# Adding four of the five feed-forward down chunks onto x inside PSUM, with ScalarE carrying x in and out

## The chip, the cores and the metric

One core of a Trainium2 chip. TensorE (PE) multiplies matrices into PSUM banks, VectorE (DVE) and ScalarE (ACT) work on tiles of 128 partitions in SBUF and PSUM, GpSimd (POOL) and SyncE (SP) mainly issue transfers. The metric is the time of one execution on the device in microseconds (us).

## The reference

A trunk of two layers over 512 tokens of width 1024. Each layer adds three things to `x`: a mixer, a memory cross-attention and a convolutional feed-forward part.

```
def conv_ffn(xn, w_up, conv_w, conv_b, w_down):
    h = causal_depthwise_conv(xn @ w_up, conv_w) + conv_b
    g, u = jnp.split(h, 2, axis=-1)
    return (jax.nn.gelu(g) * u) @ w_down

x = x + conv_ffn(rms_norm(x, ffn_norm[layer]), ...)
```

`w_up` is 1024 x 5632, `w_down` is 2816 x 1024. All is float32.

## The kernel before

`x` is kept transposed in SBUF as eight tiles `self.x[m]`, 128 features by 512 tokens each. A product of float32 precision is made of three matmuls on operands that are split into a high and a low part (`mm3`, lines 291 to 293). The split of a weight tile costs a ScalarE cast (the high part `wh`) and a VectorE subtraction (the low part `wl`).

The feed-forward part (`ffn_steps`) makes the 2816 inner features as 22 pairs of 128 gate and 128 up features. Most pairs go through `seven`: seven half products with 256 columns instead of eight (a Strassen-like scheme), whose intermediate sums sit in the PSUM banks `acc`, `y` and `s`. Between these products ScalarE carries sums from bank to bank or to SBUF: `seed` (line 1774) opens bank Y with the negative of X, `kept` (line 1778) saves two sums, lines 1791 and 1798 copy two quarters of the result out; VectorE makes the other two by a subtraction (line 1781). `tail` then applies the convolution (ScalarE line 1657, VectorE line 1664), the gelu (line 1672), the product of gate and up (line 1674) and the split of the result into `ah` (line 1678, ScalarE) and `al`. These activations stay in SBUF.

The down projection takes them in five chunks of pairs, `CHUNKS = [(0, 4), (4, 4), (8, 4), (12, 4), (16, 6)]`. As soon as a chunk of pairs is there, eight blocks `down(c, m)`, one for each output tile `m`, are put in a queue, and `fill()` takes one from it at two places of each later pair. A block loads its weights (`dr`, 256 KB), splits them (line 1554), runs 4 x 3 matmuls of 512 columns into one of the two banks `w`, and VectorE adds the bank onto `self.x[m]` (`xadd`, line 619). Pairs 0 to 4 have no down blocks in between, nor have pairs 17, 20 and 21: the last five blocks of chunk 3 are kept back and run one after the other behind the last pair. In layer 0 the eight blocks of chunk 4 follow in the same manner, with six pairs each. In layer 1 chunk 4 is left to `finish`, which adds in its own way (line 2105), loads the table for a square root (line 2133), and norms and writes the output.

The order on every engine is planned in Python. `Sched.add` takes a task's engine, estimated time, dependencies, due time and the buffers that it takes and frees. `Sched.run` gives each engine in turn the task that can start first, and among those that can start at the same time the one with the lowest due time. `clock[0]` is the running sum of TensorE's estimated time, and due times are written relative to it. Estimated times are `act = lambda n: 0.1 + 0.83e-3 * n` on ScalarE and `tt = lambda n: 0.055 + 1.06e-3 * n` on VectorE. Buffers are taken in the order of the program; the resource `w` has two slots. A framework turns the resulting program into semaphore waits and may move instructions that are ready ahead of others that are not. Each engine executes its own queue in order.

Due times that matter here: a block's weight cast at `at - 3.0`, where `at` is the clock at the block's start; the addition at the clock after the block plus 3.0; the seed of bank Y at the clock at a pair's start plus 1.5; the convolution at the clock after the pair plus 5.0 (3.0 handed to `tail`, which adds 2.0).

Of the kernel before, what the change touches and what calls it, by code (L numbers as in the profile page):

```python
# [40 lines left out]
OFF = 16  # L41
# [24 lines left out]
class Plan:  # L66
# [11 lines left out]
    def add(self, fn, dur=0.0, deps=(), prio=None, take=(), free=(), chain=(), pre=(), after=0.0, order=(), load=(), st=None):  # L78
        it = Item(fn, dur, [d for d in deps if d is not None], len(self.items) if prio is None else prio, take, free, chain, pre, after, order, load, st)
        it.n = len(self.items)  # L80
        self.items.append(it)
        return it
# [154 lines left out]
class Builder:  # L237
# [185 lines left out]
    def xs(self):  # L423
        return self.xh, self.xl
# [1082 lines left out]
    def ffn_steps(self, layer, mp):  # L1507
# [3 lines left out]
        nc, t = self.nc, self.t  # L1511
        sc = Sched(raw=3, h=3, s2=1, s4=1, a22=1, sa=3, sb=2, ra=2, hs=2, c=1, dr=2, u2=1, u5=1, act=10, acc=2, y=2, s=2, w=2)
        add = sc.add
        tt = lambda n: 0.055 + 1.06e-3 * n
        act = lambda n: 0.1 + 0.83e-3 * n
        ACV, STT = 0.71, 0.66
        clock = [0.0]
# [5 lines left out]
        def pe(dur, fn, deps, take=(), free=()):  # L1523
            clock[0] += dur
            return add("PE", dur, fn, deps, clock[0] - dur, take, free, 0.2)

        def joined(deps, prio, free):
            return add("-", 0.0, None, deps, prio, (), free, 0.0)
# [18 lines left out]
        def weight(src, cols, at, tag="raw", off=0):  # L1547

            st = {"apart": 0}
            l = load(st, tag, src, cols, at - 9.0)  # L1550

            def hi():
                st["wh"], st["wl"] = (self.til(self.wp, i, (P, 1088), F32R, bufs=3)[:, off:] for i in ("wh", "wl"))
                nc.scalar.copy(st["wh"][:, :cols], st[tag][:, :cols])  # L1554

            def low():
                n, end = st["apart"], cols - P
                for a, b, c in ((0, end, 0), (end, cols, n)) if n else ((0, cols, 0),):
                    self.sub(st["wl"][:, a + c : b + c], st[tag][:, a:b], st["wh"][:, a:b])

            def rows(k):
                s, n = slice(k * P, (k + 1) * P), k * P + (st["apart"] if (k + 1) * P == cols else 0)
                return st["wh"][:, s], st["wl"][:, n : n + P]

            st["rows"] = rows
            h = add("ACT", act(cols), hi, [l], at - 3.0, [("h", st)])
            lo = add("DVE", tt(cols), low, [h], at - 2.0, (), [(tag, st)])
            return st, lo

        def block(src, nk, xs, at, bank, deps, steps, tag="raw", off=0):  # L1570

            st, lo = weight(src, nk * P, at, tag, off)
            last = None
            per = nk // steps
            for c in range(steps):

                def fn(c=c):
                    if c == 0:
                        st["ps"] = self.bank(bank) if bank == "w" else self.acc_bank(st["_acc"] if bank == "acc" else 2 + st["_y"])
                    for k in range(c * per, (c + 1) * per):  # L1580
                        self.mm3(st["ps"][:], *st["rows"](k), *xs(k), k == 0, k == nk - 1)

                last = pe(0.7 * per, fn, [lo, last, *deps], [(bank, st)] if c == 0 else (), [("h", st)] if c == steps - 1 else ())
            return st, last

        blk = lambda k: 2 * (k % 4) + k // 4
# [33 lines left out]
        formed = []  # L1620
# [70 lines left out]
        def plain(p, fill):  # L1691
            st = {}
            at = clock[0]
            get = rows(st, at + 5.0)
            ready = []
            for j in range(2):
                b, last = block(t["up"][layer, 22 * j + p], KB8, own, clock[0], ("acc", "y")[j], (), 2)
                last.block, b["step"] = b, (16, 32)[layer]

                def evac(j=j, b=b):  # L1700
                    nc.vector.tensor_tensor(out=st["hs_"][:, j, 2:514], in0=b["ps"][:], in1=self.rb, op=ALU.mult)

                if p == 0 and j == 0:
                    nonlocal normed
                    normed = norm()
                ready.append([add("DVE", 0.6, evac, [last, get, normed], clock[0] + 2.0, (), [(("acc", "y")[j], b)])])
                fill()
            tail(p, st, ready, clock[0] + 3.0)
# [102 lines left out]
        xadded = [None] * 8  # L1811
        queue, late = [], []

        def down(c, m, steps=1):
            first, nk = CHUNKS[c]
            d, last = block(
                t[f"down{c}"][layer, m], nk, lambda k: tuple(a[:] for a in acts[first + k]), clock[0], "w", [acted[first + k] for k in range(nk)], steps,
                "dr" if nk == 4 else "raw", OFF,
            )
            last.block, d["step"] = d, 16  # L1820
            if m == 7:
                for k in range(nk):
                    joined([last], last.prio, [("act", acted[first + k].st)])
            e = add("DVE", 0.6, lambda: self.xadd(m, d["ps"]), [last, xadded[m], *formed], clock[0] + 3.0, (), [("w", d)])
            xadded[m] = e
            return e

        def fill():
            nonlocal queue
            if queue:  # L1830
                down(*queue.pop(0))
# [15 lines left out]
        if layer == 0:  # L1847
            for m in range(8):
                e = down(4, m, 2)
                a = add("ACT", 1.2, lambda m=m: self.xprep(m, "mix", 1, state), [e], clock[0] + 3.0)  # L1850
                add("DVE", 1.3, None, [a], clock[0] + 3.0)
# [428 lines left out]
```

## Time and profile before

| | |
|---|---|
| median of 3 runs | 1461.26 us (1460.26 to 1461.54) |
| profiled execution, its own time | 1460.51 us |
| its span, first to last instruction | 1458.2 us |
| mean granted TensorE clock | 0.999 |
| TensorE busy, weight loads busy | 1441.9 us, 1279.6 us |
| VectorE, ScalarE, GpSimd busy | 1258.1 us, 930.4 us, 74.8 us |
| additions onto x from a `w` bank (line 619) | 72, of 0.69 us |

The profile is one execution. Busy time is the time in which an engine had at least one instruction in work; matmuls overlap, so that TensorE can be busy throughout and still lose a little between two of them. PEld is the weight load of TensorE, which runs beside the matmuls. In rows of groups stand line, engine, operation, output and input tile, count, then busy us and mean ns, then the idle time of the engine before them and what ended it. In rows of the timeline stand start, duration, engine, line, operation, tiles and count.

### The profile page before, as it was taken

What the parts mean: (1) busy time and instruction counts of PE and PEld (TensorE: products, weight loads), DVE (VectorE), ACT (ScalarE), POOL (GpSimd) and SP (SyncE); (2) the same over time, 40 slices, a digit from 0 to 9 for tenths busy, and PEclk for the clock granted to TensorE, in tenths of its full rate; (3) what the DMA queues carried; (4) which work ended last, traced back from release to release, by engine and by line L of the source; (5) the groups of instructions that cost most, each with busy time, mean ns of one, the idle gap of its engine ahead of it and who ended that gap; (6) DMA issues with size and microseconds to landing.
All of it is one profiled execution on the core that took longest, in us unless ns stands there. A gap on an engine that the chain in (4) does not pass through costs nothing.

```text
span 1458.2 us, 24038 instructions
## 1 busy us (share of the span) xinstructions
PE 1441.9 (99%) x9019; PEld 1279.6 (88%) x9019; DVE 1258.1 (86%) x2284; ACT 930.4 (64%) x1655; POOL 74.8 (5%) x116
## 2 busy tenths in 40 slices
PE   9999999999999999999999999999999999999998
PEld 7888787998899999999888888889988999999987
DVE  7789987867899999999769988887779999999974
ACT  7689665655676656666447565566566766656654
POOL 0001120000000000000000100000000000000000
PEclk9999999999999999999999999999999999999999
DMA  5222336752245666562233331656314666565322
GB/s 200 87 74 73 121 119 206 168 171 85 95 137 153 172 172 159 154 159 71 84 101 109 116 102 65 212 136 187 131 51 121 163 172 175 152 167 152 102 68 77
DMA packets 70627, 190.23 MB, mean 130 GB/s; under 512 B 7520, under 2 KB 7520, under 8 KB 70512
## 3 DMA queue, kind: packets, MB, share of 16 engines
q1 hardware_dynamic: 62304, 161.38, 34.1%
q0 software_dynamic: 7200, 26.22, 10.8%
q8 instruction: 70, 1.15, 0.3%
q10 hardware_dynamic: 1008, 1.12, 0.2%
q14 instruction: 45, 0.37, 0.1%
HBM read 186.56 MB, written 2.13 MB: 129 GB/s over the span
## 4 chain that ended last, share of the span: by engine, by line
PE 74%; DVE 17%; ACT 4%; issue 3%; DMA 1%; POOL 0%; SPq 0%; DVEq 0%; ACTq 0%; POOLq 0%
PE acc L291 14%; PE acc L292 14%; PE acc L293 14%; PE w L291 5%; PE w L293 5%; PE w L292 5%; DVE wl L282 3%; DVE c L1664 3%; PE s L291 3%; PE s L293 3%; PE s L292 3%; PE acc L352 2%; PE acc L354 2%; PE acc L353 2%; DVE hs L1804 1%
## 5 line engine op out<-in xcount | busy, mean ns | idle before, releaser
L282 DVE TENSOR_TENSOR wl<-raw,wh 128x1024 fp32r<-128x1024 f32 (+3 forms) x181 | 214.4, 1185 | 31.2 <-ACT wh L285 28.1
L291 PE MATMUL acc<-xh,wh 128*128 128x256 f32 (+1 forms) x624 | 207.1, 332 | 0.1
L293 PE MATMUL acc<-xh,wl 128*128 128x256 f32 (+1 forms) x624 | 206.0, 330 | 0.1
L292 PE MATMUL acc<-xl,wh 128*128 128x256 f32 (+1 forms) x624 | 205.8, 330 | 0.0
L285 ACT CAST wh<-raw 128x1024 fp32r<-128x1024 f32 (+1 forms) x123 | 126.5, 1033 | 89.3 <-PE acc L292 46.8
L1664 DVE SCALAR_TENSOR_TENSOR c<-hs,vec,c 128x512 f32<-128x512 f32 x176 | 129.7, 755 | 7.2 <-ACT c L1657 5.9
L291 PEld LDWEIGHTS acc<-xh,wh 128*128 128x128 f32 x624 | 117.3, 188 | 12.0 <-ACT v L1901 0.6
L293 PEld LDWEIGHTS acc<-xh,wl 128*128 128x128 f32 x624 | 117.3, 188 | 11.9 <-DVE wl L282 0.5
L292 PEld LDWEIGHTS acc<-xl,wh 128*128 128x128 f32 x624 | 117.3, 188 | 11.6
L293 PE MATMUL w<-ah,wl 128*128 128x512 f32 x304 | 119.3, 392 | 0.0
L292 PE MATMUL w<-al,wh 128*128 128x512 f32 x304 | 118.7, 390 | 0.0
L291 PE MATMUL w<-ah,wh 128*128 128x512 f32 x304 | 118.6, 390 | 0.0
L1657 ACT ACTIVATE c<-hs,vec 128x512 f32<-128x512 f32 x88 | 69.3, 813 | 13.4 <-DVE hs L1804 11.8
L282 DVE TENSOR_TENSOR wl<-sa,wh 128x1024 fp32r<-128x1024 f32 x52 | 63.8, 1227 | 5.2 <-ACT wh L1735 3.2
L293 PEld LDWEIGHTS w<-ah,wl 128*128 128x128 f32 x304 | 57.1, 188 | 11.9
L292 PEld LDWEIGHTS w<-al,wh 128*128 128x128 f32 x304 | 57.1, 188 | 9.9
L291 PEld LDWEIGHTS w<-ah,wh 128*128 128x128 f32 x304 | 57.1, 188 | 9.8
L1735 ACT CAST wh<-sa 128x1024 fp32r<-128x1024 f32 x42 | 44.1, 1049 | 34.0 <-PE w L292 24.4
L619 DVE TENSOR_TENSOR x<-w,x 128x512 f32<-128x512 f32 x72 | 50.1, 696 | 18.0 <-PE w L293 17.8
L1554 ACT CAST wh<-dr 128x512 fp32r<-128x512 f32 x64 | 39.6, 618 | 39.0 <-issue 35.5
L1735 ACT CAST s<-sb 128x512 fp32r<-128x512 f32 x84 | 52.1, 620 | 18.7 <-PE s L293 14.7
L282 DVE TENSOR_TENSOR s<-sb,s 128x512 fp32r<-128x512 f32 x92 | 63.7, 692 | 0.3 <-ACT s L285 0.3
(533 smaller groups left out, 4643.8 us busy)
## 6 DMA issues: line engine op xcount, KB each, us to landing
raw<-in_up_dram SPq DMA_DIRECT2D x46, 512.0 KB, 3.4
sa<-in_up_dram SPq DMA_DIRECT2D x42, 512.0 KB, 3.8
sa<-in_up_dram POOLq DMA_DIRECT2D x42, 512.0 KB, 5.4
dr<-in_down_dram SPq DMA_DIRECT2D x64, 256.0 KB, 3.2
ra<-in_up_dram SPq DMA_DIRECT2D x42, 256.0 KB, 3.0
raw<-in_xk_dram SPq DMA_DIRECT2D x16, 512.0 KB, 3.4
raw<-in_wo_dram SPq DMA_DIRECT2D x16, 512.0 KB, 3.4
raw<-in_xv_dram SPq DMA_DIRECT2D x16, 512.0 KB, 3.4
```

The costliest lines, as they stand in the source:

```text
L282: self.nc.vector.tensor_tensor(out=lo, in0=v, in1=hi.bitcast(F32), op=ALU.subtract)
L285: self.nc.scalar.copy(hi, v)
L291: mm(out, wh, xh, start=first, stop=False, skip_group_check=parts)
L292: mm(out, wh, xl, start=False, stop=False, skip_group_check=parts)
L293: mm(out, wl, xh, start=False, stop=last, skip_group_check=parts)
L352: mm(ps, xh[k][:, ts], wh[:, ws], start=(k == 0), stop=False)
L353: mm(ps, xh[k][:, ts], wl[:, ws], start=False, stop=False)
L619: self.nc.vector.tensor_tensor(out=self.x[m][:], in0=ps[:], in1=self.x[m][:], op=ALU.add)
L1554: nc.scalar.copy(st["wh"][:, :cols], st[tag][:, :cols])
L1657: nc.scalar.activation(st["c_"][:, j, :], hs()[:, j, 2:514], AF.Identity, scale=self.col("cw", (layer * 3 + 2) * 44 + blk), bias=self.col( ...
L1664: nc.vector.scalar_tensor_tensor(out=c, in0=hs()[:, j, n : n + 512], scalar=w, in1=c, op0=ALU.mult, op1=ALU.add)
L1735: nc.scalar.copy(s["wh"][:, :cols], raw())
```

## The change

`block` gets an argument `onto`. With it, a ScalarE task opens the PSUM bank and copies `x[m]` into it before the block, all matmuls of the block accumulate (none has the start flag), and `down` ends with a ScalarE copy of the bank back into `x[m]` in place of VectorE's addition. This holds for chunks 0 to 3 except the first two blocks of each layer, `(0, 0)` and `(0, 1)`: 30 blocks in each layer. The bank is taken by the seed, earlier than by the first matmul. Chunk 4 keeps the addition on VectorE.

```diff
-        def block(src, nk, xs, at, bank, deps, steps, tag="raw", off=0):
+        def block(src, nk, xs, at, bank, deps, steps, tag="raw", off=0, onto=None):
 
             st, lo = weight(src, nk * P, at, tag, off)
             last = None
             per = nk // steps
+
+            def opened():
+                st["ps"] = self.bank(bank) if bank == "w" else self.acc_bank(st["_acc"] if bank == "acc" else 2 + st["_y"])
+
+            if onto is not None:
+                x, x_deps = onto
+
+                def seed():
+                    opened()
+                    nc.scalar.copy(st["ps"][:], x[:])
+
+                last = add("ACT", act(512), seed, x_deps, at - 1.5, [(bank, st)])
             for c in range(steps):
 
                 def fn(c=c):
-                    if c == 0:
-                        st["ps"] = self.bank(bank) if bank == "w" else self.acc_bank(st["_acc"] if bank == "acc" else 2 + st["_y"])
+                    if c == 0 and onto is None:
+                        opened()
                     for k in range(c * per, (c + 1) * per):
-                        self.mm3(st["ps"][:], *st["rows"](k), *xs(k), k == 0, k == nk - 1)
-
-                last = pe(0.7 * per, fn, [lo, last, *deps], [(bank, st)] if c == 0 else (), [("h", st)] if c == steps - 1 else ())
+                        self.mm3(st["ps"][:], *st["rows"](k), *xs(k), k == 0 and onto is None, k == nk - 1, onto is not None)
+
+                last = pe(0.7 * per, fn, [lo, last, *deps], [(bank, st)] if c == 0 and onto is None else (), [("h", st)] if c == steps - 1 else ())
             return st, last
...
         def down(c, m, steps=1):
             first, nk = CHUNKS[c]
+            onto = (self.x[m], [xadded[m]]) if c < 4 and (c, m) not in ((0, 0), (0, 1)) else None
             d, last = block(
                 t[f"down{c}"][layer, m], nk, lambda k: tuple(a[:] for a in acts[first + k]), clock[0], "w", [acted[first + k] for k in range(nk)], steps,
-                "dr" if nk == 4 else "raw", OFF,
+                "dr" if nk == 4 else "raw", OFF, onto,
             )
...
-            e = add("DVE", 0.6, lambda: self.xadd(m, d["ps"]), [last, xadded[m], *formed], clock[0] + 3.0, (), [("w", d)])
+            if onto is None:
+                e = add("DVE", 0.6, lambda: self.xadd(m, d["ps"]), [last, xadded[m], *formed], clock[0] + 3.0, (), [("w", d)])
+            else:
+                e = add("ACT", act(512), lambda: nc.scalar.copy(self.x[m][:], d["ps"][:]), [last, *formed], clock[0] + 1.0, (), [("w", d)])
             xadded[m] = e
             return e
```

## The prediction

> **What bounds the kernel now.** I read the page first, then the busy times by stage, then what TensorE waited for in the stage that the change touches, then the order of instructions in one of its periods and at its end.
>
> ```profile
> span 1458.2 us, 24038 instructions
> PE 1441.9 (99%) x9019; PEld 1279.6 (88%) x9019; DVE 1258.1 (86%) x2284; ACT 930.4 (64%) x1655; POOL 74.8 (5%) x116
> ```
>
> Over the whole span TensorE is busy almost without a break, but that is an average over stages. The additions that the change removes stand on L619 with a `w` bank as source, and they lie in two stretches, one for each layer. The next fence cuts these two stretches at the point where the regular interleaving of down blocks ends; its columns are length, then busy time of PE, PEld, DVE, ACT, POOL.
>
> ```profile
> 455.00:640.00 185.00, 184.68 (x1326) 172.12 (x1326) 178.59 (x282) 114.75 (x201) 10.26 (x12) 1.00 0.62 164
> 640.00:700.00 60.00, 59.58 (x462) 56.77 (x461) 55.80 (x85) 39.29 (x73) 1.81 (x3) 1.00 0.35 91
> 1160.00:1345.00 185.00, 184.84 (x1326) 172.27 (x1325) 178.61 (x281) 114.91 (x201) 11.13 (x13) 1.00 0.62 164
> 1345.00:1418.00 73.00, 72.49 (x515) 67.26 (x514) 65.04 (x98) 44.32 (x79) 0.86 (x1) 1.00 0.33 90
> sum 503.00, PE 501.58 PEld 468.42 DVE 478.04 ACT 313.27 POOL 24.05; mean PE 125.40 PEld 117.10 DVE 119.51 ACT 78.32 POOL 6.01
> ```
>
> Two things are to be seen. VectorE is at 478.04 of 503.00 us, 95%, so the stage looks short of VectorE. But TensorE is at 501.58 of 503.00: all of its idle time together is 1.42 us. The granted clock is 1.00 throughout. The waits of TensorE in the two layers, with total, count and longest, say the same:
>
> ```profile
> PE acc L291 <- DVE hs L1781: 0.2, 1, 0.2
> PE acc L291 <- ACT acc L1774: 0.2, 1, 0.2
> PE acc L291 <- ACT u L1778: 0.2, 1, 0.2
> ...
> PE acc L291 <- DVE hs L1781: 0.3, 1, 0.3
> PE acc L291 <- ACT u L1778: 0.2, 1, 0.2
> ```
>
> Five visible stalls, two ended by VectorE (0.5 us) and three by ScalarE (0.6 us); none of them stands in front of a down block.
>
> Busy time can hide short stalls, because matmuls overlap. So I look at the starts, in one period of the regular part: seven half products and two down blocks.
>
> ```profile
> 593.36 0.28 PE L291 MATMUL acc<-xh,wh 128*128 128x256 f32 x1
> 594.74 0.28 PE L291 MATMUL s<-kv,wh 128*128 128x256 f32 x1
> 596.10 0.28 PE L291 MATMUL acc<-kv,s 128*128 128x256 f32 x1
> 590.50:605.54 15.04, 15.04 (x110) 14.07 (x109) 14.23 (x24) 9.12 (x16) 0.84 (x1) 1.00 0.61 158
> ```
>
> Twelve 256-wide matmuls take 594.74 to 596.10, 1.36 us: one starts every 0.113 us and lasts 0.28, so a stall up to 0.17 us leaves no idle time. The period has 7 x 12 of these, 84 x 0.113 = 9.5 us, and 24 matmuls of twice the width, 24 x 0.227 = 5.4 us: 14.9 to 15.0 of the 15.04 us measured. TensorE is saturated by its own matmuls here. The change alters neither their number nor their shape, so all that it can save is stalls. A stall costs a little more than it shows, as one of the five does:
>
> ```profile
> 1398.91 0.38 PE L291 MATMUL acc<-kv,a 128*128 128x256 f32 x1 [0.33 <-DVE hs L1781]
> 1399.13 0.28 PE L292 MATMUL acc<-kv,a 128*128 128x256 f32 x1
> ```
>
> The matmul after it comes 0.22 us later, not 0.11. I allow the five visible stalls and as many again that are not seen, each with 0.17 us of hidden time and 0.11 of restart: 1.4 + 10 x 0.28 = 4.2 us, an estimate, is the most that can be gained, 0.3% of the kernel.
>
> **What the change removes, adds and moves.** The additions, by the busy-time view of L619 alone in the same four stretches, and the ScalarE copies that are nearest to what comes in their place (count, busy, mean ns):
>
> ```profile
> sum 503.00, DVE 41.49; mean DVE 10.37
> L1774 ACT ACTIVATE acc<-acc 128x256 f32<-128x256 f32 x42 | 15.4, 366 | 6.6 <-PE acc L293 6.6
> L1778 ACT COPY u<-acc 128x256 f32<-128x256 f32 x42 | 15.5, 370 | 13.0 <-PE acc L293 12.8
> L2055 ACT COPY num<-w 128x512 f32<-128x512 f32 x8 | 4.6, 579 | 0.8 <-PE w L2053 0.6
> L1735 ACT CAST s<-sb 128x512 fp32r<-128x512 f32 x84 | 52.1, 620 | 18.7 <-PE s L293 14.7
> ```
>
> *Removed:* of the 32 blocks of four chunks in each layer all but the first two lose their addition: 60 additions, 41.49 / 60 = 0.69 us each. VectorE falls from 478 to about 437 us, 87%. On the path: nothing, since no addition ended a wait of TensorE. At most it frees VectorE for the step that did end two of them, 0.5 us visible.
>
> *Added:* 60 copies out of the bank into x. The row for exactly this, 512 wide from a `w` bank to SBUF, is L2055: 0.579 us. And 60 copies of x into the bank. No row shows a 512-wide copy from SBUF to PSUM. L1774 against L1778 shows that at 256 wide the target makes no difference (366 against 370 ns), so I bound it by 0.579 and 0.620 us, and take 0.6. Sum 60 x (0.58 + 0.6) = 71 us of ScalarE: 313 + 71 = 384 of 503 us, 76%. ScalarE has the room; the question is only whom each copy delays.
>
> *The copy out* stands in ScalarE's queue behind the end of its block. What follows a down block is this, on ScalarE:
>
> ```profile
> 593.37 0.62 ACT L1554 CAST wh<-dr 128x512 fp32r<-128x512 f32 x1 [1.66 <-issue]
> 593.90 1.52 ACT L1657 ACTIVATE c<-hs,vec 128x512 f32<-128x512 f32 x2
> 595.32 0.36 ACT L1774 ACTIVATE acc<-acc 128x256 f32<-128x256 f32 x1
> ...
> 598.64 0.62 ACT L1678 CAST ah<-c 128x512 fp32r<-128x512 f32 x1
> 599.17 0.62 ACT L1554 CAST wh<-dr 128x512 fp32r<-128x512 f32 x1
> 599.69 0.37 ACT L1791 COPY hs<-acc 128x256 f32<-128x256 f32 x1
> ```
>
> The block ends where the next product starts, at 593.36. The copy L1774 seeds the bank of the product that starts at 596.10, and ends at 595.68: 0.42 us to spare. A copy of 0.62 us delays what stands behind it by 0.53 (598.64 to 599.17). So if the copy out went in front and nothing else moved, L1774 would end at 596.21 and TensorE would stand 0.11 us. I expect something else to move: in the planner the copy out has the due time clock + 1.0, L1774 clock + 1.5 and the two convolutions L1657 clock + 5.0. With the copy out in front, L1774 is ready by the time the first convolution ends, and goes ahead of the second. It then ends about 593.37 + 0.53 + 0.53 + 0.76 (half of the two) + 0.36 = 595.55, with 0.55 us to spare. The delayed convolution belongs to the tail of a pair whose activations are wanted many microseconds later. Cost on the path: 0; if that cover is gone, the rival below.
>
> *The seed* waits for nothing that is late: its x was written by the chunk before, its bank was freed on ScalarE itself. It becomes possible right after the copy out of the block two before, some 12 us ahead of its use (a period has two blocks), and ScalarE has 15.04 - 9.12 = 5.9 us free in the period. Cost: 0. Queued behind it are casts and product copies, each late by 0.53 at most.
>
> *At the end of the stage* this cover is thin: five down blocks follow each other with no product between them.
>
> ```profile
> 1400.42 0.39 PE L291 MATMUL w<-ah,wh 128*128 128x512 f32 x1
> 1414.07 0.39 PE L291 MATMUL acc<-ah,wh 128*128 128x512 f32 x1
> ...
> 1402.29 1.53 ACT L1657 ACTIVATE c<-hs,vec 128x512 f32<-128x512 f32 x2 [1.30 <-DVE hs L1804]
> 1403.72 0.60 ACT L1554 CAST wh<-dr 128x512 fp32r<-128x512 f32 x1
> ...
> 1409.34 0.62 ACT L1678 CAST ah<-c 128x512 fp32r<-128x512 f32 x1
> 1409.97 1.28 ACT L2133 ACT_TABLE_LOAD   x1
> ```
>
> The blocks take 13.65 / 5 = 2.73 us each. From the end of one to the start of the next but one there are 2.73 us, and in it must lie a copy out (0.58), a seed (0.6) and about 0.2 for each of two hand-overs: 1.6. Spare 1.1 us, that is two other ScalarE instructions. The third block starts at 1405.88; after the first one's end at 1403.15 ScalarE is in the second convolution until 1403.82, then copy out, cast and seed end near 1405.5. It fits, barely. Three blocks in each layer depend on such a seed; I put 0 to 0.5 us on each, take 0.1, and sum 0.6 us.
>
> **Sum.** Gain 0 to 4.2 us; I take 0.3, half of what VectorE visibly ended. Cost 0.6 us. Net +0.3 us. The profiled run took 1460.51 us, of which 2.3 lie around the span; it is 0.75 below the median of 1461.26. So 1460.8 against the profiled run, 1461.5 against the median: no difference that could be seen. About 0.2% (2.9 us) is what a measurement of this kernel can tell from no change.
>
> **The rivals.**
>
> *Faster: VectorE was the limit.* For it speaks 95% busy time, more than PEld's 93%. If so, each period shortens until TensorE alone is left, and TensorE's stalls go: up to 4.2 us, 1457.3 us. Against it speak the starts of the matmuls, which leave no room in the period. The Trainium skill (Perfetto Trace Analysis, "Identifying the Most-Contended Engine") says to judge by occupancy which engine to relieve first, and TensorE by its weight loads rather than its matmuls; by that rule VectorE at 95% is ahead of TensorE's 93%, and this change should pay. In this trace the rows of starts decide against it. Chance of over 2.9 us: 0.08.
>
> *Slower: the copy out delays the seed of the product.* If the second convolution keeps its place ahead of L1774, each period loses 0.11 us and the restart of 0.11: 0.22 x 24 periods (2 x 185 / 15.04) = 5.3 us, 1466.6 us. It decides from 0.42 us of added ScalarE work in front of L1774. For it: L1774 already stands last in its row. Against it: the due times. Chance 0.14.
>
> *Slower: the last five blocks wait for seeds.* If two more instructions get between, or the table load (1.28 us), a seed is late by 0.5 to 1.0 us; six of them, 3 to 6 us: about 1465. For it: thin spare time. Against it: the first convolutions are over early, and the bank's release is never on another engine. Chance 0.10.
>
> That the change doesn't do what it says (the seeds' order leaving all in place, or more than 60 blocks) would show in the count of L619; it would make no other time than the forecast.
>
> **How the numbers follow.** Forecast, stalls only moved about: 0.68, time 1461.5, its own range 1459.5 to 1463.5. The faster rival 0.08; the slower ones 0.14 and 0.10, together 0.24. The range must leave out no more than 0.2: it begins at 1459.0, which cuts off the faster rival, and reaches to 1466.6, which takes in both slower ones up to their prices. Faster by over 0.2% 0.08, within 0.68, slower 0.24.
>
> **What would show it.** Right: L619 with source `w` falls from 72 to 12; VectorE's busy time in the stage falls by about 41 us and ScalarE's rises by about 71; TensorE's busy time stays within a few us of the length of each stretch; the period stays 15.04 us; L1774 stands between the two convolutions. Wrong: a wait of `PE w L291` for ScalarE of over 0.3 us each at the five last blocks (late seeds), a period of 15.2 us or more with `PE acc L291 <- ACT acc L1774` in it (the product's seed), or a period below 15.0 us (VectorE had been the limit after all).

## The result: 0.19% faster, just outside the range

| | before | after |
|---|---|---|
| median (21 runs each, side by side) | 1461.54 us | 1458.72 us |
| profiled execution, its own time | 1460.51 us | 1458.72 us |
| its span | 1458.2 us | 1456.9 us |

The ratio of the two is 0.9981, interval [0.9975, 0.9987]: 2.8 us less, between 1.9 and 3.7. The forecast was 1461.5 us in a range from 1459.0 to 1466.6. The result lies 0.28 us below that range, and it is clear of no change.

The page of the changed kernel, first its span and then the busy time of each engine:

```profile
span 1456.9 us, 24068 instructions
PE 1440.6 (99%) x9019; PEld 1277.7 (88%) x9019; DVE 1225.9 (84%) x2224; ACT 985.5 (68%) x1775; POOL 72.9 (5%) x116
```

The two stretches of the feed-forward part by busy time, as before (the last one ends 1 us earlier, because the stage does):

```profile
455.00:640.00 185.00, 184.89 (x1329) 172.26 (x1328) 167.48 (x260) 135.31 (x246) 10.24 (x12) 1.00 0.63 164
640.00:700.00 60.00, 59.56 (x466) 56.87 (x465) 54.88 (x82) 43.41 (x82) 1.81 (x3) 1.00 0.37 93
1160.00:1345.00 185.00, 184.88 (x1328) 172.29 (x1327) 167.51 (x259) 135.33 (x246) 11.13 (x13) 1.00 0.63 164
1345.00:1417.00 72.00, 71.55 (x511) 66.35 (x510) 60.37 (x90) 51.44 (x94) 0.86 (x1) 1.00 0.34 89
sum 502.00, PE 500.88 PEld 467.77 DVE 450.25 ACT 365.49 POOL 24.04; mean PE 125.22 PEld 116.94 DVE 112.56 ACT 91.37 POOL 6.01
```

VectorE went from 478 to 450 us, ScalarE from 313 to 365. TensorE's idle time went from 1.42 to 1.12 us. That is a small difference beside 2.8 us, so busy time again doesn't show where the time came from. The waits of TensorE show part of it. In the same stretches (455 to 700 and 1160 to 1418) one is listed in each layer:

```profile
PE acc L291 <- DVE hs L1793: 0.3, 1, 0.3
...
PE acc L291 <- DVE hs L1793: 0.3, 1, 0.3
```

The waits for VectorE are still there (line 1781 of before is 1793 now; lines 1575 to 1815 moved by 12, those behind 1824 by 16). The three that ScalarE had ended, L1774 and twice L1778, are no longer listed. Waits under 0.15 us are left out of this list; the starts of the matmuls show some of them below. The change put 120 instructions on ScalarE, and the listed waits that went were ScalarE's. The timeline shows how for the first of them. In the kernel before, ScalarE and then TensorE:

```profile
518.93 1.52 ACT L1657 ACTIVATE c<-hs,vec 128x512 f32<-128x512 f32 x2 [0.64 <-DVE hs L1804]
520.36 0.36 ACT L1774 ACTIVATE acc<-acc 128x256 f32<-128x256 f32 x1
...
520.29 0.28 PE L293 MATMUL s<-kv,wl 128*128 128x256 f32 x1
520.78 0.38 PE L291 MATMUL acc<-kv,s 128*128 128x256 f32 x1 [0.21 <-ACT acc L1774]
```

The same place in the changed kernel:

```profile
519.12 0.81 ACT L1669 ACTIVATE c<-hs,vec 128x512 f32<-128x512 f32 x1
519.84 0.57 ACT L1840 COPY x<-w 128x512 f32<-128x512 f32 x1
520.31 0.38 ACT L1786 ACTIVATE acc<-acc 128x256 f32<-128x256 f32 x1
520.61 0.58 ACT L1584 COPY w<-x 128x512 f32<-128x512 f32 x1
521.11 0.82 ACT L1669 ACTIVATE c<-hs,vec 128x512 f32<-128x512 f32 x1
...
521.26 0.28 PE L293 MATMUL s<-kv,wl 128*128 128x256 f32 x1
521.37 0.28 PE L291 MATMUL acc<-kv,s 128*128 128x256 f32 x1
```

Before, the two convolutions run as a pair, VectorE's L1804 releases them late, and the seed of bank Y (L1774) stands behind both. The matmul that needs it starts 0.49 us after its predecessor instead of 0.11. After, the copy out stands behind the first convolution; the seed of bank Y (L1786) is ready by then, comes next, and ends at 520.69. The matmul starts at 521.37, so there are 0.68 us to spare. ScalarE's order is not the only thing that differs here. Before, L1804 ends 0.14 us ahead of the product `s` in front of the stall (518.90 and 519.04). After, the same instruction (L1816) ends 0.99 us ahead of it (519.02 and 520.01). So VectorE's result also comes earlier in relation to TensorE.

The second place is the wait for the saved sum, L1778, at 644.28. VectorE, ScalarE and TensorE before:

```profile
640.72 2.73 DVE L1664 SCALAR_TENSOR_TENSOR c<-hs,vec,c 128x512 f32<-128x512 f32 x4
...
640.47 0.80 ACT L1657 ACTIVATE c<-hs,vec 128x512 f32<-128x512 f32 x1
642.82 0.63 ACT L1672 ACTIVATE c<-c 128x512 f32<-128x512 f32 x1 [1.03 <-DVE c L1664]
643.87 0.36 ACT L1778 COPY u<-acc 128x256 f32<-128x256 f32 x1
...
644.28 0.39 PE L291 MATMUL acc<-kv,wh 128*128 128x256 f32 x1 [0.18 <-ACT u L1778]
```

and after, ScalarE and TensorE:

```profile
641.86 0.83 ACT L1669 ACTIVATE c<-hs,vec 128x512 f32<-128x512 f32 x1
642.83 0.65 ACT L1684 ACTIVATE c<-c 128x512 f32<-128x512 f32 x1
643.88 0.38 ACT L1790 COPY u<-acc 128x256 f32<-128x256 f32 x1
...
644.41 0.28 PE L291 MATMUL acc<-kv,wh 128*128 128x256 f32 x1
```

The gelu (L1672) needs the two taps of the gate half. Before, the second convolution ends at 641.27, VectorE takes a tap of each half in turn, and the gelu waits 1.03 us for the third of the four. The saved sum stands behind it. After, the copy out (640.59) and the copy of x (641.36) stand between the convolutions. The second one ends at 642.69, VectorE does both taps of the gate first, and the gelu doesn't wait. In relation to the product that needs the saved sum, that sum is ready 0.4 us earlier, and this wait is gone. Here it is ScalarE's order that changed VectorE's, and relief alone (adds_out below) leaves the wait as it was.

Matching the matmuls of the two traces in order and comparing their starts, I can say what each part of the run gained. Both feed-forward stages are shorter in the profiled run of after: by 0.80 us from 395 to 720 in layer 0, and by 0.89 from 1100 to 1414 in layer 1 (times of before). The last part gained 0.3. A step of +0.96 us at 264 lies ahead of everything that the change touches; a shift up to there of +0.4 to +2.1 us is in the profiles of five of the ten kernels below too, so it isn't the change's.

Stalls are less than half of the 1.7 us in the two stages. The matmuls that start late by over 0.08 us (in 455 to 700 and 1160 to 1418) lose about 0.7 us less in after. The rest is something that neither busy time nor the list of waits shows. These are the first matmuls of two products of twelve, in before and then in after:

```profile
650.04 0.28 PE L291 MATMUL s<-kv,wh 128*128 128x256 f32 x1
651.45 0.28 PE L291 MATMUL acc<-kv,s 128*128 128x256 f32 x1
...
649.86 0.28 PE L291 MATMUL s<-kv,wh 128*128 128x256 f32 x1
651.22 0.28 PE L291 MATMUL acc<-kv,s 128*128 128x256 f32 x1
```

Twelve matmuls take 1.41 us in before and 1.36 in after: one every 0.118 us in place of 0.113. In before this goes on from the stall at 644.28 to 654, seven products long, and costs 0.4 us. Such slow stretches add up to about 0.9 us more in before's two stages than in after's. The granted clock is 1.00 in them too. Their cause is not shown. Most follow a stall, but not every stall has one behind it (none at 520.78), and at least one is not the change's doing: before's profile has one from 292 to 300, ahead of everything that the change touches, and after's has none there. So this part of the gain in these two profiles may in part be chance.

### The profile page after: what moved, and what is told of

Its sections match the earlier page's. It is cut to its first block, busy times and chain, and to the rows that moved or that the text cites. A ratio compares the mean times of both kernels' runs of the same rounds, so it can differ in the third digit from the quotient of the medians.

```text
span 1456.9 us, 24068 instructions
## 1 busy us (share of the span) xinstructions
PE 1440.6 (99%) x9019; PEld 1277.7 (88%) x9019; DVE 1225.9 (84%) x2224; ACT 985.5 (68%) x1775; POOL 72.9 (5%) x116
## 3 DMA queue, kind: packets, MB, share of 16 engines
q8 instruction: 70, 1.15, 0.3%
q10 hardware_dynamic: 1008, 1.12, 0.2%
## 4 chain that ended last, share of the span: by engine, by line
PE 82%; DVE 10%; ACT 4%; issue 2%; DMA 2%; SPq 0%; POOL 0%; ACTq 0%; DVEq 0%; POOLq 0%
PE acc L291 15%; PE acc L292 14%; PE acc L293 14%; PE w L293 6%; PE w L291 6%; PE w L292 6%; PE s L293 3%; PE s L291 3%; PE s L292 3%; PE acc L352 2%; PE acc L354 2%; PE acc L353 2%; DVE wl L282 2%; DMA sa<-in_xq_dram 1%; DVE x L771 1%
## 5 line engine op out<-in xcount | busy, mean ns | idle before, releaser
L1676 DVE SCALAR_TENSOR_TENSOR c<-hs,vec,c 128x512 f32<-128x512 f32 x176 | 130.4, 749 | 16.0 <-ACT c L1669 14.0
L1732 POOL DMA_DIRECT2D sa<-in_up_dram x42 | 35.9, 855 | 516.5 <-DVE wl L282 184.5
L291 PE MATMUL acc<-mem,wh 128*128 128x256 f32 (+1 forms) x192 | 61.5, 320 | 0.0
```

The costliest lines, as they stand in the source:

```text
L291: mm(out, wh, xh, start=first, stop=False, skip_group_check=parts)
L1676: nc.vector.scalar_tensor_tensor(out=c, in0=hs()[:, j, n : n + 512], scalar=w, in1=c, op0=ALU.mult, op1=ALU.add)
L1732: return add("POOL", 0.0029 * cols, lambda: nc.gpsimd.dma_start(out(), src(), accum_op=ALU.add), deps, due, (), (), 6.0)
```

## The experiments

Each was timed in 11 runs beside the kernel before on the same chip (after_keep in 10). The last two columns are the change in length of the two feed-forward stages, in us, between the profiled run and before's.

| kernel | additions on VectorE | copies out, ScalarE | x into the bank | ratio to before | layer 0 | layer 1 |
|---|---|---|---|---|---|---|
| after | 12 | 60 | ScalarE | 0.9981 [0.9975, 0.9987] | -0.80 | -0.89 |
| load_back | 12 + 60 useless | 60 | ScalarE | 1.0022 [1.0013, 1.0031] | +2.06 | +2.23 |
| adds_out | 12 | none | none | 0.9993 [0.9984, 1.0002] | -0.27 | -0.71 |
| act_copy | 72 | 60 useless | none | 0.9991 [0.9982, 1.0] | +0.33 | -0.95 |
| hold | 72 | none | none | 0.9994 [0.9985, 1.0003] | -0.14 | -0.32 |
| act_copy_fill | 72 | 50 useless | none | 0.9986 [0.9977, 0.9994] | -0.74 | -0.92 |
| seed_dve | 12 | 60 | VectorE | 0.9999 [0.9991, 1.0008] | +0.49 | +0.50 |
| before_keep | 72 | none | none | 0.9991 [0.9983, 1.0] | -0.35 | -0.81 |
| after_keep | 12 | 60 | ScalarE | 0.998 [0.9971, 0.9989] | -1.15 | -0.98 |
| no_seed | 12 | 60 | none | 0.9984 [0.9975, 0.9993] | -0.47 | -0.62 |
| after_mix | 22 | 50 | ScalarE | 0.998 [0.9972, 0.9989] | -0.76 | -0.86 |

An interval is 1.2 to 1.3 us to either side (0.9 for after). Distances from before are worked out from the ratio. The medians of before were 1461.27 us beside the first four experiments, 1461.95 beside the next four and 1461.96 beside the last two; distances between medians are up to 0.9 us larger. The sums of the two stages lie 0 to 1.3 us above what the ratios say. They are all taken against one profile of before, whose own time was about 1 us below its median, and each profile has its own slow stretches.

The first four experiments set theory A (the copy out changes ScalarE's order, and that removes the stalls) against theory B (VectorE's relief removes them).

**load_back**: the work taken from VectorE is given back as additions that nobody uses.

```diff
             e = add("ACT", ..., lambda: nc.scalar.copy(self.x[m][:], d["ps"][:]), [last, *formed], clock[0] + 1.0, ...)
+            add("DVE", 0.6, lambda: nc.vector.tensor_tensor(out=scratch, in0=h, in1=h, op=ALU.add), [last, *formed], clock[0] + 3.0)
```

> The changed kernel, and after each of the 60 blocks VectorE does an addition of the same size again (of SBUF operands into a scratch tile, with the due time of the removed one). VectorE's load is that of before, ScalarE's that of after. Theory A (the two new ScalarE copies change the order on ScalarE, so that the copies that TensorE waits for come earlier; VectorE's relief plays no part): still 2 to 3 us below before. Theory B (VectorE had 32 us taken off, so that its results reach ScalarE earlier): back to within 0.7 us of before.

Measured: 1464.48 us, 3.2 above before. Both theories missed it. Two new stalls of 0.56 or 0.57 us stand in each layer. This is one of them, VectorE first, then ScalarE, then TensorE:

```profile
551.91 0.69 DVE L1844 TENSOR_TENSOR sqt<-xh 128x512 f32<-128x512 f32 x1
552.52 0.75 DVE L1676 SCALAR_TENSOR_TENSOR c<-hs,vec,c 128x512 f32<-128x512 f32 x1
553.18 0.69 DVE L1844 TENSOR_TENSOR sqt<-xh 128x512 f32<-128x512 f32 x1
553.78 1.41 DVE L1676 SCALAR_TENSOR_TENSOR c<-hs,vec,c 128x512 f32<-128x512 f32 x2
...
554.57 0.63 ACT L1684 ACTIVATE c<-c 128x512 f32<-128x512 f32 x1 [0.72 <-DVE c L1676]
555.11 0.60 ACT L1747 CAST s<-sb 128x512 fp32r<-128x512 f32 x1
555.61 0.37 ACT L1790 COPY u<-acc 128x256 f32<-128x256 f32 x1
...
556.03 0.39 PE L291 MATMUL acc<-kv,wh 128*128 128x256 f32 x1 [0.57 <-ACT u L1790]
```

VectorE does a useless addition between the convolution's taps (L1676). The gelu (L1684) waits for them at the head of ScalarE's queue, and a cast and the saved sum (L1790), which TensorE needs, stand behind it. So VectorE reaches TensorE by way of ScalarE's queue, and the wait is written down to ScalarE. The useless additions come bunched, here two between taps within 1.3 us; the real ones in the kernel before came 5.0 to 9.7 us apart. How much is the load and how much the bunching, this run doesn't separate.

**adds_out**: the kernel before without those 60 additions and with nothing in their place.

```diff
-            e = add("DVE", 0.6, lambda: self.xadd(m, d["ps"]), ...)
+            e = joined([last], clock[0], [("w", d)])
```

> The kernel before with the 60 additions left out and nothing in their place (x lacks these blocks). VectorE is relieved as in the change, ScalarE has nothing new. Theory A: within 0.7 us of before. Theory B: 2 to 3 us below before, or more.

Measured: 1459.65 us, about 1 us below before and not clear of zero. Relief alone removes the stall at 520.78 (VectorE's L1804 is earlier, so both convolutions are) and leaves the two at L1778 (0.18 us at 643.69 and 1347.29).

**act_copy**: the additions stay, and ScalarE copies the bank to a place that nobody reads, at the due time of the copy out. The addition waits for that copy (`j` among its dependencies).

```diff
+                j = add("ACT", act(512), lambda: nc.scalar.copy(scratch, d["ps"][:]), [last, *formed], clock[0] + 1.0)
-                e = add("DVE", 0.6, ..., [last, xadded[m], *formed], clock[0] + 3.0, (), [("w", d)])
+                e = add("DVE", 0.6, ..., [last, j, xadded[m], *formed], clock[0] + 3.0, (), [("w", d)])
```

> The kernel before, all additions on VectorE, and one ScalarE copy of the bank into a scratch tile after each of the 60 blocks, with the due time of the change's copy out. More work, nothing relieved. Theory A: the same place in ScalarE's order is taken by this copy, so 1 to 2.5 us below before. Theory B: not faster, 0 to 2 us slower.

Measured: 1460.12 us, 1.3 below before, the interval touching 1. The interleaved part gains 0.78 us up to 697. Then the last five blocks of layer 0 lose 1.1, since there the bank now passes from ScalarE to VectorE before it is free:

```profile
711.31 0.47 PE L291 MATMUL w<-ah,wh 128*128 128x512 f32 x1 [0.88 <-DVE x L619]
```

**hold**: one order is imposed on the kernel before, the second convolution behind the seed of bank Y.

```diff
+                with self.tc.issue_after(state["seed"].ins) if j and "seed" in state else ExitStack():
                     nc.scalar.activation(st["c_"][:, j, :], hs()[:, j, 2:514], AF.Identity, ...)
```

> The kernel before with one order edge: the second convolution of a pair is issued on ScalarE behind the latest seed of a product's bank Y. No work is added or moved. Theory A: the stalls in front of the product that this seed opens go, 0.8 us in both layers together, those behind the copies of saved sums stay: 0.5 to 1.5 us below before. Theory B: no change within 0.5 us.

Measured: 1460.26 us, 0.9 below, not clear of zero. The stall at 520.78 is gone, and this is the run in which nothing but an order on ScalarE was imposed. But the edge costs something too: a wait for the seed of bank Y in a pair without down blocks, 0.3 us before, is now 0.7 (at 449.56 and 1153.37).

The next four set theory C (ScalarE's order in the interleaved part is the gain) against theory D (VectorE's relief is needed).

**act_copy_fill**: act_copy, but with no copies in the last five blocks.

```diff
-            if c == 4 or (c, m) in ((0, 0), (0, 1)):
+            if c == 4 or (c, m) in ((0, 0), (0, 1)) or (c == 3 and m >= 3):
                 # as before the change
```

> The kernel before with the additional ScalarE copy of the bank into a scratch tile, as in the run with such copies, but not for the five blocks at the end of chunk 3. Theory C (the gain is ScalarE's order in the interleaved stretch, where the copy out takes its place): the stalls in front of Y's product and behind the saved sum at pair 17 go, 1.7 us in the trace, 1.0 to 2.4 us in the median. Theory D (VectorE's relief is needed): within 0.7 us of before.

Measured: 1459.82 us, 2.0 below before (0.9 to 3.4). VectorE is nearly as full as before (473 of 503 us against 478), and ScalarE has 23 us more, all of it useless:

```profile
519.01 0.58 ACT L1827 COPY sqt<-w 128x512 f32<-128x512 f32 x1
519.49 0.82 ACT L1657 ACTIVATE c<-hs,vec 128x512 f32<-128x512 f32 x1
520.21 0.37 ACT L1774 ACTIVATE acc<-acc 128x256 f32<-128x256 f32 x1
520.51 0.80 ACT L1657 ACTIVATE c<-hs,vec 128x512 f32<-128x512 f32 x1
...
sum 503.00, PE 501.88 PEld 469.02 DVE 473.15 ACT 336.72 POOL 24.54; mean PE 125.47 PEld 117.25 DVE 118.29 ACT 84.18 POOL 6.13
```

The seed of bank Y stands between the convolutions, as in after. This run says that less work on VectorE is not needed for a gain. It doesn't say that ScalarE's order alone gives it. Since the additions wait for the copies, most come 3.2 or 4.4 us behind their block in place of 2.0, so VectorE's order changed as well. L1804 ends at 518.92 here, 0.94 us ahead of the product `s` (519.86), against 0.14 in before. The waits differ too. Those at 520.78 and 644.28 are gone, and so are the two for L1781 at the end of the stages (694.82, 1398.91), but one of 0.35 us has come at 648.80, for L1781 again, and the matmul at 654.63 starts 0.39 us late in place of 0.09.

**seed_dve**: the changed kernel, but VectorE copies x into the bank.

```diff
-                    nc.scalar.copy(st["ps"][:], x[:])
+                    nc.vector.tensor_copy(st["ps"][:], x[:])
-                last = add("ACT", act(512), seed, x_deps, at - 1.5, [(bank, st)])
+                last = add("DVE", 0.6, seed, x_deps, at - 1.5, [(bank, st)])
```

> The changed kernel with one part given back: VectorE copies x into the bank, ScalarE still copies the sum out. VectorE has 60 copies in place of 60 additions, so it is hardly relieved. Theory C: the copy out keeps its place in ScalarE's order, so 1.5 to 3 us below before. Theory D: within 0.7 us of before.

Measured: 1461.89 us, no difference from before. Theory C missed it, and theory D's bound held. A stall for the seed of bank Y is back, in another period and in both layers:

```profile
474.63 0.38 PE L291 MATMUL acc<-kv,s 128*128 128x256 f32 x1 [0.23 <-ACT acc L1786]
...
1179.06 0.38 PE L291 MATMUL acc<-kv,s 128*128 128x256 f32 x1 [0.23 <-ACT acc L1786]
```

**before_keep** and **after_keep**: the kernel before and the changed one, with the order of the plan kept around four instructions (seed of bank Y, both saved sums, the first subtraction): what is planned behind them on ScalarE or VectorE is issued behind them.

```diff
+        first = {}
         for t in done:
             if t.fn:
-                t.fn()
+                with self.tc.issue_after(first[t.eng]) if t.eng in first else ExitStack():
+                    made = t.fn()
+                if t.lead:
+                    first[t.eng] = made.ins
```

> The kernel before with order edges only: on ScalarE and VectorE every feed-forward instruction that the planner put behind one of the steps that TensorE waits for (the seed of Y, the two saved sums, the first subtraction) is issued behind it. No work is added or moved. Theory C: at least what the change gives, 2 to 4 us below before. Theory D: at most 1 us below.

> The changed kernel with the same order edges. Theory C: much the same as the edges on the kernel before, within 1 us of it, since both then have TensorE's steps first. Theory D: 2 us or more below the edges on the kernel before.

Measured: 1460.16 us (1.3 below before, interval touching 1) and 1458.2 us (2.9 below). With the order kept in both, the change is still worth 1.6 us by the ratios (2.0 between the medians). That lies between what the theories said (C at most 1, D at least 2), and the two intervals overlap, so it decides nothing. after_keep isn't to be told apart from after (0.998 against 0.9981). Its one listed stall in each layer (from 455 and from 1160 on) is another one, `acc` waiting 0.5 us for the seed of bank Y.

The last two asked what the seeds cost.

**no_seed**: the changed kernel without the copies of x into the bank.

```diff
-                "dr" if nk == 4 else "raw", OFF, onto,
+                "dr" if nk == 4 else "raw", OFF, None,
```

> The changed kernel, but no x is copied into the bank: the first matmul of the block opens it, and ScalarE's copy out writes the block's sum over x (the addition of x is left out of the result). So VectorE is relieved, the copy out stands where it stood, and 60 copies of 0.58 us are gone from ScalarE. Theory E (the seed on ScalarE costs something that the relief of VectorE only covers): faster than the changed kernel by 1 us or more, ratio to the kernel before 0.9965 to 0.9975. Theory F (the seed costs nothing, gains by the copy out's place and by the relief overlap): the same as the changed kernel, ratio 0.998, within 0.0007.

Measured: 1459.19 us, ratio 0.9984. Theory F: 60 copies fewer on ScalarE gain nothing that can be measured. Beside seed_dve (0.9999), which has the same copies out and 60 copies of x on VectorE, this kernel is 2.2 us faster, though the two intervals still touch: there the copies of x seem to cost.

**after_mix**: the last five blocks of each layer as before the change.

```diff
-            onto = (self.x[m], [xadded[m]]) if c < 4 and (c, m) not in ((0, 0), (0, 1)) else None
+            onto = (self.x[m], [xadded[m]]) if c < 4 and (c, m) not in ((0, 0), (0, 1)) and not (c == 3 and m >= 3) else None
```

> The changed kernel, but the last five blocks of four chunks of each layer (the ones that follow each other) are as before the change: no seed, addition on VectorE. My prediction's term for late seeds (0.6 us over six blocks) would make this kernel 0.6 us faster than the changed one, ratio to the kernel before about 0.9977. If late seeds cost nothing, as the changed kernel's profile shows at the end of its second layer, it is the same or up to 0.5 us slower, ratio 0.998 to 0.9985.

Measured: 1458.51 us, ratio 0.998, the same as after. A cost of the late seeds of 0.6 us would be smaller than this interval; none is seen.

## Why the prediction was wrong, point by point

**What failed: the gain of 0.3 us, and the step that set it, "On the path: nothing, since no addition ended a wait of TensorE".** The prediction had the right kind of ceiling (only stalls can be gained), and its list had three stalls ended by ScalarE and two by VectorE. It counted only VectorE's as reachable, because VectorE was the engine that got relief, and took half of them. The opposite happened. VectorE's two visible stalls are still there. Of ScalarE's, the one at 520.78 cost 0.49 us with its restart, those at 644.28 and 1348.37 cost 0.45 each, and all three are gone. Both kinds go back to VectorE through ScalarE's queue: the convolution in front of L1774 waited for L1804, and the gelu in front of L1778 waited for VectorE's taps. The prediction's own paragraph on the copy out had half of the mechanism, L1774 ahead of the second convolution, but used it only to price the copy at nothing. It had not asked what the same reorder does at the places where that seed was late already, and the wait for L1774 stood in its own fence. The net change measured 1.9 to 3.7 us down, in place of 0.3 up. In the profiled runs 2.0 us of it are placed: 0.80 and 0.89 in the stages and 0.3 behind them. About half of what the stages gained is the slow spacing of matmuls, for which the prediction's 0.28 us for each stall had no term. The rest, up to the 2.8 between the medians, is not placed.

**Why it moved, as far as shown.** Useless copies, on a kernel whose VectorE does all its additions but does them later, give 2.0 us (act_copy_fill). Relief alone gives 1.0, not clear of zero (adds_out). Relief and the copy out together give 2.3 (no_seed), and with the seeds 2.8 (after); these intervals overlap. The parts do not add, and the trace shows why at one place. The stall at 520.78 goes if an order holds the second convolution back (hold), or if VectorE is early enough to release the convolutions (adds_out). In after, no_seed and act_copy_fill both are so: the seed stands between the convolutions, and VectorE's result comes 0.9 us or more ahead of the product `s`. Either is enough. At 644.28 relief alone is not enough, and the changed order is. Relief matters when something else is added: with x copied in by VectorE the gain is gone (seed_dve), and with the additions given back it turned into a loss of 3.2 us (load_back). How the 2.8 us split between order and relief stays open, how much of it is slow spacing stays open, and so does what in load_back is the load.

**Late seeds, 0.6 us: too much.** The end of the stage in layer 1, ScalarE and then TensorE:

```profile
1407.21 1.28 ACT L2149 ACT_TABLE_LOAD   x1
...
1408.70 0.57 ACT L1840 COPY x<-w 128x512 f32<-128x512 f32 x1
...
1409.90 0.59 ACT L1584 COPY w<-x 128x512 f32<-128x512 f32 x1
...
1410.38 0.40 PE L291 MATMUL acc<-ah,wh 128*128 128x512 f32 x1
1410.61 0.43 PE L291 MATMUL w<-ah,wh 128*128 128x512 f32 x1
```

The table load did get in front, as the second slower rival had it, and the last seed ends at 1410.49, after the block could have begun. But TensorE has a matmul of the next product ready (`acc`, 1410.38), and puts it in the gap. The last block starts 0.23 us late for it, and the next product later has that matmul done already, so TensorE loses almost nothing. after_mix agrees within its interval. The prediction had put the seeds of the interleaved part at nothing. There they do cost a little: at 478.32 a copy of x (0.58 us) stands in front of a saved sum, and the matmul that needs that sum starts at 479.26, 0.28 us after its predecessor in place of 0.11. The same is seen at 1182.59.

**Durations, counts and places: right. Busy times: too large.** The seed was bounded by 0.579 and 0.620 us and the copy out was put at 0.579:

```profile
L1584 ACT COPY w<-x 128x512 f32<-128x512 f32 x60 | 35.0, 584 | 1.0
...
L1840 ACT COPY x<-w 128x512 f32<-128x512 f32 x60 | 34.4, 574 | 0.0
...
L619 DVE TENSOR_TENSOR x<-w,x 128x512 f32<-128x512 f32 x12 | 8.2, 683 | 9.2 <-PE w L293 9.2
```

L619 from a `w` bank fell from 72 to 12. VectorE's busy time fell by 28 us in place of 41, and ScalarE's rose by 52 in place of 71: in part because instructions that follow each other overlap (519.12 + 0.81 is 519.93, and the next starts at 519.84), so a sum of durations is not the busy time. The period stayed:

```profile
590.50:605.54 15.04, 15.04 (x110) 14.06 (x109) 13.14 (x21) 10.96 (x21) 0.84 (x1) 1.00 0.61 160
```

In this period the copy out stands behind the first convolution and not in front of it, as had been expected, and the seed of bank Y comes next. Its spare time was put at 0.55 us; it is 0.69 (from 595.88 to the product's start at 596.57).

**The rivals.** No wait for the seed of bank Y is listed in the two stretches of after: the first slower rival is out, and for the reason given, since that seed goes ahead of the second convolution. The second slower rival met its condition and not its price. The faster rival had the sign right and the cause wrong: with all 60 additions gone (adds_out) the kernel gains 1.0 us, interval 2.3 to -0.3, and not 4.2. By the rule in the Trainium skill (Perfetto Trace Analysis, "Identifying the Most-Contended Engine") VectorE's 95% was the thing to relieve. No run here bears that out by itself, since adds_out is not clear of zero. A gain of 2.0 us came with VectorE at 473 of 503 us and ScalarE fuller than before. But load_back shows that VectorE's lateness is not harmless.

**The range.** Its lower end was set at 1459.0 to cut off a rival that was thought to need VectorE as the limit. That is 2.5 us below the forecast, which is just the price of the five visible stalls by the prediction's own figures (1.1 + 5 x 0.28). The stalls that can't be seen, 1.7 us more up to its ceiling, were left out. Every stall is a place where the time can go down as well as up, whatever the engine that is relieved, and the range should have reached to the ceiling. That the time stayed within 0.2% of before, to which the prediction gave its largest chance, was luck: the change is 2.8 us, and 0.2% are 2.9.

## What to carry to other kernels

When a stage is saturated, list the stalls with what each waits for, and ask of every added or moved instruction whether it changes the order in front of one of them, on whatever engine, for better as well as for worse. Look at the spacing of the starts as well as at the waits, since matmuls can lose time with no gap between them. A wait is written down to the last engine in the chain; follow it back through that engine's queue, because the cause may stand on another. And when single edits do not add up, as here, look for one stall that several of them remove.

## What was not expected

Useless work made the kernel faster: 50 copies of 0.58 us on ScalarE, read by nobody, gave a ratio of 0.9986 [0.9977, 0.9994]. They change which ready instruction comes next on ScalarE and, since the additions wait for them, on VectorE. The same kind of useless work on VectorE, 60 additions of 0.69 us, cost 6 us against the changed kernel (1.0022 against 0.9981), with two stalls of 0.57 us to be seen in each layer. By the starts of the matmuls each of these costs 0.84 us (0.73, and 0.11 at the next), 3.4 us together; the rest lies in smaller stalls and slow spacing and isn't added up here. Slow spacing itself was not expected: at a granted clock of 1.00, 256-wide matmuls that start every 0.113 us start every 0.118 for 10 us and more, often behind a stall. A copy of 512 columns takes 584 ns into PSUM and 574 ns out of it, so the target made no difference on ScalarE at this width.
